# Sums of squares queued one by one between projection products, and a norm's factors spread over the partitions through DRAM

## The chip, the core and the metric

The kernel runs on one core of a Trainium2 chip. The core has five engines with instruction streams of their own: TensorE (PE in the profile, with its weight loads listed as PEld), VectorE (DVE), ScalarE (ACT), GpSimd (POOL) and SyncE (SP), which issues the DMAs of this kernel. They meet through semaphores. The metric is the time of one execution on the device in microseconds (us), as the median of several runs.

## The reference

One inference step of a trunk of two layers over 1152 tokens: 128 context tokens and 1024 latent ones, 9 tiles of 128. A layer normalises its input, projects it, runs three branches (A: windowed attention, B: a linear recurrence, C: differential attention) and merges them. The change touches the end of branch C's heads (4 in a layer, `DV_C` = 128):

```python
def block(qblk):
    s = jnp.einsum('bqhmd,bshmd->bhmqs', qblk, k).astype(jnp.float32) * SCALE
    p = jax.nn.softmax(s, axis=-1)
    pd = p[:, :, 0] - lam * p[:, :, 1]
    return jnp.einsum('bhqs,bshe->bqhe', pd.astype(v.dtype), v)

o = jnp.moveaxis(lax.map(block, qb), 0, 1).reshape(B, T, H_C, DV_C)
o = rmsnorm(o, subln) * (1 - lam_init)
...
oc * jax.nn.silu(g_c)     # the branch's gate, ahead of its output projection
```

Each head's output, a row of 128 numbers for each token, is divided by its root mean square, multiplied by the vector `subln` and a constant, and then by the gate.

## The kernel before

**Layout.** A head's output `u.o` (named `O` in the trace) lies with the 128 features on the partitions and the 1152 tokens along them. The sum of squares of a token therefore runs over the partitions, which a matmul with a column of ones does; it gives nine columns of 128 tokens, tokens on the partitions. The factors have to come back the other way: for each token the same number on all 128 partitions.

**Order.** The unit phase of a layer (`unit_phase`) runs heads 0 to 3 of branch C and then branch A. Each head goes through groups of query tiles: the context tile alone, then pairs of latent tiles. For a group, `q_conv` turns the queries over (transposes L415 into PSUM, ACT and DVE split the result in two halves, `qhl`), `c_probs` makes the scores of a tile (two maps, three blocks of 384 keys each; L513 and L514 on TensorE into `ps_s`), DVE empties each block and takes its maximum (L515), ACT takes exponentials (L525), and DVE joins the two maps (L106). `c_pv`, run a group later from `flush`, transposes the probabilities (L542), ACT and DVE split them (`PT`, L94 and L97), and TensorE multiplies them with the values (`ps_o`, L158 to L160). All of this is written with `tc.high_priority` (offset `HPO` = 2000).

Between groups, `step(n)` advances a generator, `background()`, which feeds projection products for the next head: `tok_gemm` and `ws_chunk` run eight k-steps of `mm3` (three products at L158, L159 and L160, `ps_s<-uwh,h` and `ps_s<-uwl,h`) into one `ps_s` buffer. They fill TensorE while the softmax runs. A scheduler orders the instructions of each engine by priority and dependence, and each engine then runs its own list in that order. Each tile takes a buffer from a ring named by a tag: PSUM has four buffers `s`, three `t` and one `o`; in SBUF the ring `T` (which holds `PT`) has two, `S` 26 and `P` 7.

**A head's end.** `c_finish` (L553 to L571) runs from `flush`, two tiles into the next head. ACT squares `u.o` into `sq` (L555, a `T` buffer). Nine matmuls (L558, `ps_t<-one,sq`, 128 partitions by one column, each two instructions in the trace) make the sums. `rsqrt` runs about a dozen small steps on DVE (`rsq`, 128x9). Nine matmuls with the identity (L566, `ps_t<-ident,rsq`, also two instructions each) spread the factors to all partitions, three to a PSUM buffer. DVE multiplies `u.o` with `subln` and those factors, read from PSUM (L106, called from L568, three of 384 columns), POOL multiplies by the gate, and a DMA on SP's queue stores the head to DRAM (`osp`). Other names that come up: `qkraw`, `qktmp` and `qkss` are the norm of the next head's keys (squares at L365 on ACT, a reduction at L366 on DVE); `qdup` is a doubled copy of the queries (one half by DVE at L410, one by ACT).

Of the kernel before, what the change touches and what calls it, by code (L numbers as in the profile page):

```python
# [10 lines left out]
F32 = mybir.dt.float32  # L11
# [3 lines left out]
ALU = mybir.AluOpType  # L15
# [3 lines left out]
DEPTH = 2  # L19
NTOK = 1152  # L20
NT = 9
KT = 8
# [2 lines left out]

HPO = 2000
TPO = 1500

MLAG = 1
LAG2 = (7, 8)  # L30
# [28 lines left out]
def hybrid_dit_kernel(ctx, tc, I, O):  # L59
# [4 lines left out]
    drp = ctx.enter_context(tc.tile_pool(name="dr", bufs=1, space=bass.MemoryType.DRAM))  # L64
# [3 lines left out]
    def ps(tag, *shape):  # L68
        return psp.tile([128] + list(shape), F32, tag=tag, name="ps_" + tag, bufs=PSB[tag])
# [4 lines left out]
    def al(tag, name, *shape):  # L74

        return big.tile([128] + list(shape), F32, tag=tag, name=name, bufs=RINGS[tag])

    def r(ap):
        return ap.bitcast(F32R)
# [10 lines left out]
    def dma(out, in_):  # L90
        nc.sync.dma_start(out=out, in_=in_)

    def acopy(out, in_, scale=1.0):
        A.activation(out=out, in_=in_, func=AF.Copy, scale=scale)  # L94

    def tt(e, out, a, b, op):
        e.tensor_tensor(out=out, in0=a, in1=b, op=op)  # L97
# [7 lines left out]
    def stt(out, a, s, b, op0, op1):  # L105
        V.scalar_tensor_tensor(out=out, in0=a, scalar=s, in1=b, op0=op0, op1=op1)  # L106

    ident = tl("ident", 128)
    one = tl("one", 1)


    xres = drp.tile([NT, 128, DM], F32, name="xres")
    osp = [drp.tile([4, 128, NTOK], F32, name=f"osp{b}") for b in range(3)]
    xsp, gsp = (drp.tile([4, 128, NTOK], F32, name=n) for n in ("xsp", "gsp"))
    ysp = drp.tile([8, 128, NTOK], F32, name="ysp")
# [3 lines left out]
    def rsqrt(x, n, scale, eps=None):  # L119

        o = tl("rsq", 4, 12, bufs=3)
        ms, y, h, t = (o[:, i, 0:n] for i in range(4))
        if eps is None:
            ts(V, ms, x, scale, ALU.mult, EPS, ALU.add)
        else:
            stt(ms, x, scale, eps, ALU.mult, ALU.add)
        ts(V, y.bitcast(I32), ms.bitcast(I32), 1, ALU.logical_shift_right)
        ts(V, y.bitcast(I32), y.bitcast(I32), -1.0, ALU.mult, float(0x5F3759DF), ALU.add)
        ts(V, h, ms, -0.5, ALU.mult)
        for _ in range(3):  # L130
            tt(V, t, y, y, ALU.mult)
            tt(V, t, t, h, ALU.mult)
            stt(y, t, 1.5, y, ALU.add, ALU.mult)
        return y
# [22 lines left out]
    def mm3(out, lh, ll, rh, rl, first, last):  # L157
        T.matmul(out=out, lhsT=r(lh), rhs=r(rh), start=first, stop=False)  # L158
        T.matmul(out=out, lhsT=r(lh), rhs=r(rl), start=False, stop=False)  # L159
        T.matmul(out=out, lhsT=r(ll), rhs=r(rh), start=False, stop=last)  # L160

    class Lay:
        pass
# [1 line left out]
    def hchunk(L, c, k):  # L165
        return L.hh[k][:, 3 * c:3 * c + 3, :], L.hl[k][:, 3 * c:3 * c + 3, :]

    def ws_chunk(L, hi, lo, c):
        p = ps("s", 384)
        for k in range(KT):  # L170
            a, b = hchunk(L, c, k)
            mm3(p, hi[:, k, :], lo[:, k, :], a, b, k == 0, k == KT - 1)
        return p

    def ws_gemm(L, wcols, consume):
# [173 lines left out]
    def tok_gemm(L, i, w):  # L349
        p = ps("s", 384)  # L350
        for k in range(KT):
            mm3(p, L.hh[k][:, i, :], L.hl[k][:, i, :], w[k][0], w[k][1], k == 0, k == KT - 1)
        return p

    def qk_rows(L, i0, pss, gains, dsts, eng=None):
# [195 lines left out]
        acopy(u.o[:, tiles[0] * 128:tiles[0] * 128 + w], po)  # L551

    def c_finish(L, u, h):  # L553
        sq = al("T", "sq", 1152)
        A.activation(out=sq, in_=u.o, func=AF.Square)  # L555
        p = ps("t", 9)
        for i in range(9):
            T.matmul(out=p[:, i:i + 1], lhsT=sq[:, i * 128:(i + 1) * 128], rhs=one, start=True, stop=True)  # L558
        e2 = tl("e2", 9)
        stt(e2, u.l0, EPS, u.l0, ALU.mult, ALU.mult)  # L560
        y = rsqrt(p, 9, 1.0 / 128, e2)
        for c in range(3):
            pb = ps("t", 3, 128)
            for t in range(3):
                i = 3 * c + t
                T.matmul(out=pb[:, t, :], lhsT=y[:, i:i + 1].to_broadcast([128, 128]), rhs=ident, start=True, stop=True)  # L566
            oc = u.o[:, c * 384:(c + 1) * 384].rearrange("p (t n) -> p t n", t=3)
            stt(oc, oc, L.D.sub1, pb, ALU.mult, ALU.mult)  # L568
            tt(Pq, u.o[:, c * 384:(c + 1) * 384], u.o[:, c * 384:(c + 1) * 384],
               u.gate[:, c * 384:(c + 1) * 384], ALU.mult)  # L570
        dma(osp[2][h], u.o)  # L571

# [126 lines left out]
    def unit_phase(L):  # L701
# [1 line left out]
        l = L.l  # L703
        a_groups = [CQA, CKA, CVA]
        pend = None

        done = None

        def flush():
            nonlocal pend, done  # L710
            d, done = done, None
            if pend:
                pend()
                pend = None
            if d:
                d()

        def start(h):
            u = Unit()
# [21 lines left out]
        def step(n):  # L741
            for _ in range(n):
                next(bg, None)

        def fg(f, *args):
            with tc.high_priority(offset=HPO):
# [431 lines left out]
    for l in range(DEPTH):  # L1178
        L = Lay()
        L.l = l  # L1180
        L.yr, L.ssq, L.units, L.y, L.gates, L.late = [None] * 8, [], [], [], [], []
        L.o = {br: [] for br in range(3)}
        Ls.append(L)

    def drive(*gens):
# [129 lines left out]
```

## Time and profile before

| | |
|---|---|
| median of three runs | 2838.39 us (2835.95 to 2838.65) |
| the profiled execution's own time | 2841.75 us |
| its span in the profile | 2840.0 us |
| mean granted TensorE clock | 0.984 of full speed |
| TensorE busy | 2731.5 us, 96% |
| VectorE busy | 1792.6 us, 63% |
| ScalarE busy | 1285.3 us, 45% |
| GpSimd busy | 923.9 us, 33% |

The rows further down come from one profiled execution. A busy time is the union of an engine's instructions. Matmuls are pipelined: an instruction's listed duration overlaps with the next one's, so the step from one start to the next tells what it costs in a stream. A clock of 1.00 is 2.4 GHz for TensorE; the other level is 1.2 GHz, so a stretch with a mean of 0.90 ran a fifth of its time at that.

### The profile page before, as it was taken

What the parts mean: (1) busy time and instruction counts of PE and PEld (TensorE: products, weight loads), DVE (VectorE), ACT (ScalarE), POOL (GpSimd) and SP (SyncE); (2) the same over time, 40 slices, a digit from 0 to 9 for tenths busy, and PEclk for the clock granted to TensorE, in tenths of its full rate; (3) what the DMA queues carried; (4) which work ended last, traced back from release to release, by engine and by line L of the source; (5) the groups of instructions that cost most, each with busy time, mean ns of one, the idle gap of its engine ahead of it and who ended that gap; (6) DMA issues with size and microseconds to landing.
All of it is one profiled execution on the core that took longest, in us unless ns stands there. A gap on an engine that the chain in (4) does not pass through costs nothing.

```text
span 2840.0 us, 44370 instructions
## 1 busy us (share of the span) xinstructions
PE 2731.5 (96%) x16745; PEld 2640.8 (93%) x16745; DVE 1792.6 (63%) x4412; ACT 1285.3 (45%) x2577; POOL 923.9 (33%) x756
## 2 busy tenths in 40 slices
PE   8999999999999999999999999999999998999999
PEld 4889999999999999999989899999999998999999
DVE  5897878775634675824858887887766257612262
ACT  4464554566635651122244555555666266512200
POOL 1333344541223552122204343445312245512230
PEclk9999999999999999999999999999999999999999
DMA  6010011111222344623531010111122223423232
GB/s 231 26 33 29 24 33 34 35 55 51 89 92 75 112 158 152 199 70 114 173 104 34 24 34 20 33 49 32 49 71 71 90 92 101 163 87 106 76 110 83
DMA packets 240852, 228.52 MB, mean 80 GB/s; under 512 B 22706, under 2 KB 218620, under 8 KB 240636
## 3 DMA queue, kind: packets, MB, share of 16 engines
q1 hardware_dynamic: 240636, 225.67, 24.7%
q8 instruction: 132, 2.16, 0.3%
q14 instruction: 84, 0.69, 0.1%
HBM read 172.40 MB, written 53.22 MB: 79 GB/s over the span
## 4 chain that ended last, share of the span: by engine, by line
PE 73%; DVE 13%; ACT 4%; issue 4%; POOL 2%; DMA 2%; SPq 1%; DVEq 0%; ACTq 0%; POOLq 0%
PE ps_s L158 17%; PE ps_s L159 17%; PE ps_s L160 17%; PE ps_o L159 2%; PE ps_o L158 2%; PE ps_o L160 2%; PE ps_o L684 2%; PE ps_t L675 2%; DVE P L515 2%; PE ps_s L513 2%; PE ps_t L542 2%; PE ps_s L514 1%; DVE lr L907 1%; PE ps_s L635 1%; DVE P L106 1%
## 5 line engine op out<-in xcount | busy, mean ns | idle before, releaser
L158 PE MATMUL ps_s<-h,wsh 128*128 128x384 f32 x1440 | 489.5, 343 | 10.3 <-ACT mg L1005 5.6
L160 PE MATMUL ps_s<-h,wsl 128*128 128x384 f32 x1440 | 485.8, 341 | 1.0 <-POOL wsl L97 1.0
L159 PE MATMUL ps_s<-h,wsh 128*128 128x384 f32 x1440 | 485.8, 340 | 0.0
L97 POOL TENSOR_TENSOR wsl<-wsraw,wsh 128x1024 fp32r<-128x1024 f32 x80 | 199.8, 2497 | 357.5 <-ACT wsh L94 167.1
L158 PEld LDWEIGHTS ps_s<-h,wsh 128*128 128x128 f32 x1440 | 272.0, 189 | 13.6 <-ACT mg L1005 6.6
L160 PEld LDWEIGHTS ps_s<-h,wsl 128*128 128x128 f32 x1440 | 271.3, 189 | 1.9 <-POOL wsl L97 1.6
L159 PEld LDWEIGHTS ps_s<-h,wsh 128*128 128x128 f32 x1440 | 272.1, 189 | 0.3
L97 POOL TENSOR_TENSOR qkraw<-qkraw,tab 128x384 f32<-128x384 f32 (+2 forms) x92 | 132.0, 1446 | 338.7 <-DVE qkraw L97 216.6
L515 DVE TENSOR_SCALAR_CACHE_REDUCE P<-ps_s 128x384 f32<-128x384 f32 (+1 forms) x400 | 205.8, 540 | 38.7 <-PE ps_s L514 37.7
L97 DVE TENSOR_TENSOR PT<-ps_t,PT 128x512 fp32r<-128x512 f32 (+2 forms) x304 | 187.8, 626 | 61.6 <-ACT PT L94 60.0
L158 PE MATMUL ps_s<-uwh,h 128*128 128x384 f32 x648 | 222.7, 345 | 2.9 <-ACT h L94 1.9
L159 PE MATMUL ps_s<-uwl,h 128*128 128x384 f32 x648 | 220.6, 342 | 0.0
L160 PE MATMUL ps_s<-uwh,h 128*128 128x384 f32 x648 | 218.5, 345 | 0.0
L94 ACT ACTIVATE PT<-ps_t 128x512 fp32r<-128x512 f32 (+2 forms) x304 | 159.7, 546 | 127.3 <-PE ps_o L160 69.4
L525 ACT ACTIVATE P<-P,csm 128x1152 f32<-128x1152 f32 (+1 forms) x144 | 165.9, 1155 | 96.0 <-DVE csm L101 96.0
L158 PE MATMUL ps_s<-yh,wsh 128*128 128x384 f32 x480 | 164.0, 347 | 14.9 <-ACT mg L1005 10.2
L1005 ACT ACTIVATE mg<-ps_s 128x384 f32<-128x384 f32 x144 | 69.2, 486 | 239.4 <-DVE ps_s L106 122.6
L158 PE MATMUL ps_s<-woh,yh 128*128 128x256 f32 x576 | 164.0, 286 | 0.0
L160 PE MATMUL ps_s<-yh,wsl 128*128 128x384 f32 x480 | 163.0, 342 | 1.0 <-POOL wsl L97 1.0
L160 PE MATMUL ps_s<-woh,yl 128*128 128x256 f32 x576 | 163.8, 285 | 0.0
L159 PE MATMUL ps_s<-wol,yh 128*128 128x256 f32 x576 | 163.6, 284 | 0.0
L159 PE MATMUL ps_s<-yl,wsh 128*128 128x384 f32 x480 | 162.1, 341 | 0.0
(276 smaller groups left out, 7374.5 us busy)
## 6 DMA issues: line engine op xcount, KB each, us to landing
wsraw<-in_w_in_dram SPq DMA_DIRECT2D x80, 512.0 KB, 4.3
ysp<-yr SPq DMA_DIRECT2D x32, 576.0 KB, 5.6
yr<-ysp SPq DMA_DIRECT2D x32, 576.0 KB, 5.4
wuraw<-in_w_in_dram SPq DMA_DIRECT2D x72, 192.0 KB, 3.9
ol<-osp SPq DMA_DIRECT2D x24, 576.0 KB, 4.9
modw<-in_mod_w_dram SPq DMA_DIRECT2D x20, 576.0 KB, 6.1
modw<-in_mod_w_dram SPq DMA_DIRECT2D x16, 512.0 KB, 5.5
woraw<-in_w_out_dram SPq DMA_DIRECT2D x16, 512.0 KB, 3.4
```

The costliest lines, as they stand in the source:

```text
L94: A.activation(out=out, in_=in_, func=AF.Copy, scale=scale)
L97: e.tensor_tensor(out=out, in0=a, in1=b, op=op)
L158: T.matmul(out=out, lhsT=r(lh), rhs=r(rh), start=first, stop=False)
L159: T.matmul(out=out, lhsT=r(lh), rhs=r(rl), start=False, stop=False)
L160: T.matmul(out=out, lhsT=r(ll), rhs=r(rh), start=False, stop=last)
L513: T.matmul(out=p, lhsT=qh, rhs=kk, start=True, stop=False)
L515: V.tensor_scalar(out=S[:, n * c:n * c + n], in0=p, scalar1=1.0, scalar2=NEG, op0=ALU.mult, op1=ALU.max, accum_out=mx[:, mp, c:c + 1])
L525: A.activation(out=Ss[mp][:, 0:n], in_=Ss[mp][:, 0:n], func=AF.Exp, scale=0.125, bias=nm[:, mp:mp + 1], accum_out=acc)
L542: T.transpose(p[:, b, j * 128:(j + 1) * 128], Pm[:, (b0 + b) * 128:(b0 + b + 1) * 128], ident)
L675: T.transpose(p[:, b, 128 * j:128 * j + 128], Ps[2 * t + j][:, (b0 + b) * 128:(b0 + b + 1) * 128], ident)
L684: T.matmul(out=po[:, t, :, :], lhsT=r(vs[kb]), rhs=r(x[:, b, :]), start=kb + k == 0, stop=k == 1 and kb == len(vs) - 1)
L1005: A.activation(out=m, in_=p, func=AF.Tanh, scale=0.5)
```

## The change

The squares `sq` take a buffer of ring `S` (heads 0 to 2) or `P` (head 3) in place of `T`. The nine sums are no longer written at once: each goes into a list, `L.small`, and a new function `between` takes one out after each k-step of `tok_gemm` and `ws_chunk`; `tc.issue_after` holds it behind the product that was just written. `c_finish` becomes a generator in three parts, advanced one part for each `step` at a priority offset `NPO` = 300, or run to its end by the next `flush`. After the root, the factors are turned by one transpose (9 rows of 128 tokens), copied by ACT into the first nine partitions of `sq`, stored to DRAM (`ybd`, 4.6 KB) and loaded back from there into all of `sq`, the same 1152 numbers to each of 128 partitions (576 KB in SBUF). Both DMAs are on SP's queue. The DVE multiplies then read their factors from `sq` in SBUF. The arithmetic is the same.

```diff
-            mm3(p, hi[:, k, :], lo[:, k, :], a, b, k == 0, k == KT - 1)
+            mm = mm3(p, hi[:, k, :], lo[:, k, :], a, b, k == 0, k == KT - 1)
+            between(L, mm)
...
-            mm3(p, L.hh[k][:, i, :], L.hl[k][:, i, :], w[k][0], w[k][1], k == 0, k == KT - 1)
+            mm = mm3(p, L.hh[k][:, i, :], L.hl[k][:, i, :], w[k][0], w[k][1], k == 0, k == KT - 1)
+            between(L, mm)
...
+    def between(L, mm=None):
+
+        if L.small and mm is not None:
+            with tc.issue_after(mm.ins):
+                L.small.pop(0)()
+        elif L.small:
+            L.small.pop(0)()
...
     def c_finish(L, u, h):
-        sq = al("T", "sq", 1152)
+
+        sq = al("S" if h < 3 else "P", "sq", NTOK)
         A.activation(out=sq, in_=u.o, func=AF.Square)
         p = ps("t", 9)
+
+        def total(i):
+            T.matmul(out=p[:, i:i + 1], lhsT=sq[:, i * 128:(i + 1) * 128], rhs=one, start=True, stop=True)
         for i in range(9):
-            T.matmul(out=p[:, i:i + 1], lhsT=sq[:, i * 128:(i + 1) * 128], rhs=one, start=True, stop=True)
+            L.small.append(lambda i=i: total(i))
+        yield
+        while L.small:
+            between(L)
         e2 = tl("e2", 9)
         stt(e2, u.l0, EPS, u.l0, ALU.mult, ALU.mult)
         y = rsqrt(p, 9, 1.0 / 128, e2)
+        yd = ybd[4 * L.l + h]
+
+        def turn():
+            p = ps("t", 128)
+            T.transpose(p[0:9, :], y, ident)
+            acopy(sq[0:9, 0:128], p[0:9, :])
+            dma(yd, sq[0:9, 0:128])
+            dma(sq.rearrange("p (t n) -> p t n", n=128), yd[None].to_broadcast([128, 9, 128]))
+        L.small += [lambda: None, lambda: None, lambda: None, turn]
+        yield
+        while L.small:
+            between(L)
         for c in range(3):
-            pb = ps("t", 3, 128)
-            for t in range(3):
-                i = 3 * c + t
-                T.matmul(out=pb[:, t, :], lhsT=y[:, i:i + 1].to_broadcast([128, 128]), rhs=ident, start=True, stop=True)
-            oc = u.o[:, c * 384:(c + 1) * 384].rearrange("p (t n) -> p t n", t=3)
-            stt(oc, oc, L.D.sub1, pb, ALU.mult, ALU.mult)
-            tt(Pq, u.o[:, c * 384:(c + 1) * 384], u.o[:, c * 384:(c + 1) * 384],
-               u.gate[:, c * 384:(c + 1) * 384], ALU.mult)
+            cs = slice(384 * c, 384 * c + 384)
+            stt(u.o[:, cs], u.o[:, cs], L.D.sub1, sq[:, cs], ALU.mult, ALU.mult)
+            tt(Pq, u.o[:, cs], u.o[:, cs], u.gate[:, cs], ALU.mult)
         dma(osp[2][h], u.o)
+        yield
...
             if d:
-                d()
+                for _ in fin:
+                    pass
+                fin = d() or iter(())
+                next(fin, None)
...
             for _ in range(n):
                 next(bg, None)
+                with tc.high_priority(offset=NPO):
+                    next(fin, None)
```

The scheduler then places the pieces. The listings below are instructions in the order in which an engine runs them, with the line, the operation and `out<-in`; lines after the change are numbered otherwise (L158 to L160 become L161 to L163, L513 and L514 become L526 and L527, L558 becomes L573, L542 becomes L555). Heads 0 to 2 of both layers have one pattern.

TensorE from the last value product of head 0 of the first layer (`ps_o<-PT,xkv`) on, before the change; `one,sq` are the sums, `uwh,h` and `uwl,h` projection products:

```order
L160 MATMUL ps_o<-PT,xkv 128x128
L558 MATMUL ps_t<-one,sq 128x1 x4
L513 MATMUL ps_s<-ck,qhl 128x384
L558 MATMUL ps_t<-one,sq 128x1
L514 MATMUL ps_s<-ck,qhl 128x384
L558 MATMUL ps_t<-one,sq 128x1 x4
L513 MATMUL ps_s<-ck,qhl 128x384
...
L158 MATMUL ps_s<-uwh,h 128x384
L566 MATMUL ps_t<-ident,rsq 128x128 x9
L159 MATMUL ps_s<-uwl,h 128x384
```

TensorE in the same place after the change, from the last score product to the transpose of the factors:

```order
L527 MATMUL ps_s<-ck,qhl 128x384
L161 MATMUL ps_s<-uwh,h 128x384
L162 MATMUL ps_s<-uwl,h 128x384
L163 MATMUL ps_s<-uwh,h 128x384
L573 MATMUL ps_t<-one,sq 128x1
...
L573 MATMUL ps_t<-one,sq 128x1 x2
...
L163 MATMUL ps_s<-uwh,h 128x384
L586 MATMUL ps_t<-ident,rsq 9x128
L428 MATMUL ps_t<-ident,qdup 128x128
L555 MATMUL ps_t<-ident,P 128x128 x3
```

The sums have moved from the scores to places behind three projection products each, and the nine broadcasts, which stood eleven projection products before the next tiles, have become one transpose that stands behind the last projection product.

ACT at the start of the next group, before the change; the two first rows are the ends of projections, `qktmp` are the squares of the next head's keys:

```order
L94 ACTIVATE uvr<-ps_s 128x128
L94 ACTIVATE qkraw<-ps_s 128x256
L94 ACTIVATE qhl<-ps_t 128x512
L94 ACTIVATE qdup<-uq 128x4x64
L365 ACTIVATE qktmp<-qkraw 128x768
L94 ACTIVATE PT<-ps_t 128x512 x4
```

ACT in the same place after the change:

```order
L96 ACTIVATE uvr<-ps_s 128x128
L96 ACTIVATE qkraw<-ps_s 128x256
L96 ACTIVATE sq<-ps_t 9x128
L378 ACTIVATE qktmp<-qkraw 128x768
L96 ACTIVATE PT<-ps_t 128x512
L96 ACTIVATE qhl<-ps_t 128x512
L96 ACTIVATE qdup<-uq 128x4x64
```

The copy of the turned factors stands first, and the queries' half `qhl` stands behind the squares and a half of the probabilities, where it stood ahead of both.

DVE in the same stretch, before the change; the multiplies by the factors are `O<-O,sub_530,ps_t`:

```order
L106 SCALAR_TENSOR_TENSOR P<-P,csm 128x1152
L106 SCALAR_TENSOR_TENSOR O<-O,sub_530,ps_t 128x384 x3
L410 COPY qdup<-uq 128x4x64
L97 TENSOR_TENSOR qhl<-ps_t,qhl 128x512
L366 TENSOR_REDUCE qkss<-qktmp 128x12
L515 TENSOR_SCALAR P,csm<-ps_s 128x384 x3
```

DVE in the same stretch after the change, where they are `O<-O,sub_531,sq`:

```order
L423 COPY qdup<-uq 128x4x64
L379 TENSOR_REDUCE qkss<-qktmp 128x12
L99 TENSOR_TENSOR PT<-ps_t,PT 128x512
L99 TENSOR_TENSOR qhl<-ps_t,qhl 128x512
...
L99 TENSOR_TENSOR PT<-ps_t,PT 128x512
...
L528 TENSOR_SCALAR P,csm<-ps_s 128x384
L108 SCALAR_TENSOR_TENSOR O<-O,sub_531,sq 128x384 x2
L528 TENSOR_SCALAR P,csm<-ps_s 128x384
L108 SCALAR_TENSOR_TENSOR O<-O,sub_531,sq 128x384
```

The three multiplies have moved from ahead of the copy of the queries to places behind the first and the second emptied block of the next scores.

TensorE at the end of head 3, where branch A follows, before the change:

```order
L558 MATMUL ps_t<-one,sq 128x1 x9
L158 MATMUL ps_s<-uwh,h 128x384
L159 MATMUL ps_s<-uwl,h 128x384
L160 MATMUL ps_s<-uwh,h 128x384
...
L566 MATMUL ps_t<-ident,rsq 128x128 x9
L415 MATMUL ps_t<-ident,qdup 128x128 x4
```

TensorE at the end of head 3 after the change:

```order
L573 MATMUL ps_t<-one,sq 128x1 x9
L162 MATMUL ps_s<-uwl,h 128x384
L163 MATMUL ps_s<-uwh,h 128x384
L586 MATMUL ps_t<-ident,rsq 9x128
L428 MATMUL ps_t<-ident,qdup 128x128
```

Here the nine sums stay in one run; two projection products are left between them and the transpose, where six stood ahead of the broadcasts.

## Rows read from the trace of the kernel before

**Rows 1.** The page: each engine's busy us, share, instructions

```profile
PE 2731.5 (96%) x16745; PEld 2640.8 (93%) x16745; DVE 1792.6 (63%) x4412; ACT 1285.3 (45%) x2577; POOL 923.9 (33%) x756
```

**Rows 2.** Windows, stretches A: span, busy us (instructions) by engine, clock, DMA share

```profile
225.20:243.10 17.90, 17.61 (x102) 16.34 (x101) 13.81 (x50) 6.05 (x12) 8.90 (x15) 0.90 0.01 4
...
1834.40:1850.80 16.40, 16.07 (x102) 15.06 (x101) 13.44 (x50) 5.93 (x12) 8.78 (x15) 1.00 0.02 5
sum 101.90, PE 100.23 PEld 95.40 DVE 81.95 ACT 35.78 POOL 52.91; mean PE 16.71 PEld 15.90 DVE 13.66 ACT 5.96 POOL 8.82
```

**Rows 3.** Windows, the same columns, stretches B

```profile
243.10:253.50 10.40, 10.15 (x71) 9.09 (x69) 9.14 (x31) 4.73 (x11) 0.90 (x1) 1.00 0.15 59
...
1651.20:1662.40 11.20, 11.20 (x85) 11.07 (x83) 10.37 (x35) 5.53 (x12) 1.04 (x2) 1.00 0.16 60
...
sum 63.30, PE 62.05 PEld 56.68 DVE 56.55 ACT 29.35 POOL 5.65; mean PE 10.34 PEld 9.45 DVE 9.42 ACT 4.89 POOL 0.94
```

**Rows 4.** Timeline of TensorE, head 0: start, us, line, op, out<-in, count

```profile
223.13 0.28 PE L158 MATMUL ps_o<-PT,uv 128*128 128x256 f32 x1
223.25 0.28 PE L159 MATMUL ps_o<-PT,uv 128*128 128x256 f32 x1
...
226.33 0.42 PE L513 MATMUL ps_s<-ck,qhl 128*128 128x384 f32 x1
...
226.73 0.42 PE L514 MATMUL ps_s<-ck,qhl 128*128 128x384 f32 x1
...
232.68 0.44 PE L158 MATMUL ps_s<-uwh,h 128*128 128x384 f32 x1
...
239.21 2.17 PE L566 MATMUL ps_t<-ident,rsq 128*128 128x128 f32 x18
241.13 0.42 PE L159 MATMUL ps_s<-uwl,h 128*128 128x384 f32 x1
...
243.13 0.60 PE L415 MATMUL ps_t<-ident,qdup 128*128 128x128 f32 x4
```

**Rows 5.** Timeline of VectorE, head 0

```profile
224.65 0.55 DVE L515 TENSOR_SCALAR_CACHE_REDUCE P<-ps_s 128x384 f32<-128x384 f32 x1
...
225.12 0.55 DVE L515 TENSOR_SCALAR_CACHE_REDUCE P<-ps_s 128x384 f32<-128x384 f32 x1
...
240.29 1.74 DVE L106 SCALAR_TENSOR_TENSOR O<-O,sub,ps_t 128x384 f32<-128x384 f32 x3
```

**Rows 6.** Timeline of all engines, start of stretch B of head 0

```profile
243.76 0.60 ACT L94 ACTIVATE qhl<-ps_t 128x512 fp32r<-128x512 f32 x1
...
244.42 0.97 PE L513 MATMUL ps_s<-ck,qhl 128*128 128x384 f32 x4
244.56 0.84 ACT L365 ACTIVATE qktmp<-qkraw 128x768 f32<-128x768 f32 x1
...
245.30 1.08 ACT L94 ACTIVATE PT<-ps_t 128x512 fp32r<-128x512 f32 x2
245.43 0.95 DVE L366 TENSOR_REDUCE qkss<-qktmp 128x12 f32<-128x768 f32 x1 [0.34 <-ACT qktmp L365]
```

**Rows 7.** DMA issues: out<-in, queue, count, KB each, median us to landing

```profile
ol<-osp SPq DMA_DIRECT2D x24, 576.0 KB, 4.9
...
osp<-O SPq DMA_DIRECT2D x8, 576.0 KB, 2.9
...
out_dram<-uvr SPq DMA_DIRECT2D x10, 64.0 KB, 1.5
```

**Rows 8.** Timeline, end of head 3, both layers; in brackets the wait before

```profile
534.95 0.17 DVE L106 SCALAR_TENSOR_TENSOR rsq<-ps_t,e 128x9 f32<-128x9 f32 x1 [1.95 <-PE ps_t L558]
...
537.51 2.27 PE L566 MATMUL ps_t<-ident,rsq 128*128 128x128 f32 x18 [1.45 <-DVE rsq L106]
537.58 0.96 DVE L97 TENSOR_TENSOR qkraw<-qkraw,rsq 128x768 f32<-128x768 f32 x1
...
1941.25 3.90 PE L566 MATMUL ps_t<-ident,rsq 128*128 128x128 f32 x18 [1.45 <-DVE rsq L106]
```

More of the change, by code (lines that the diff above doesn't have):

```diff
@@ L27 @@
 TPO = 1500
+NPO = 300
 MLAG = 1
@@ L112, in hybrid_dit_kernel @@
     xres = drp.tile([NT, 128, DM], F32, name="xres")
+    ybd = drp.tile([4 * DEPTH, NT, 128], F32, name="ybd")
     osp = [drp.tile([4, 128, NTOK], F32, name=f"osp{b}") for b in range(3)]
@@ L159, in mm3 @@
         T.matmul(out=out, lhsT=r(lh), rhs=r(rl), start=False, stop=False)
-        T.matmul(out=out, lhsT=r(ll), rhs=r(rh), start=False, stop=last)
+        return T.matmul(out=out, lhsT=r(ll), rhs=r(rh), start=False, stop=last)
     class Lay:
@@ L707, in unit_phase @@
         done = None
+        fin = iter(())
         def flush():
-            nonlocal pend, done
+            nonlocal pend, done, fin
             d, done = done, None
@@ L1182, in hybrid_dit_kernel @@
         L.o = {br: [] for br in range(3)}
+        L.small = []
         Ls.append(L)
```

## The prediction

> **What bounds the kernel now.** I read the page's busy times first: TensorE is busy 2731.5 of 2840.0 us [rows 1], so time is saved where TensorE does less, runs at the lower clock less or waits less, and lost where it gets a new wait. Then I cut each of heads 0 to 2 in both layers into two stretches. **Stretch A** runs from the finished head's last value product to the last projection product before the next tiles; it holds the 24 score products of two tiles (12 blocks), the sums, 48 projection products and the broadcasts. **Stretch B** follows, up to the next projection product: scores and value products of the next two tiles. Six stretches A take 101.9 us, and four of the six have a granted clock of 0.90, the other two 1.00 [rows 2]: 0.90 over 17.9 us is some 3.6 us at 1.2 GHz instead of 2.4. Six stretches B take 63.3 us with TensorE busy for 62.05 of them, all at 1.00 [rows 3]. So A has something to give; B has no slack that a new wait could use.
>
> Within A the timeline of TensorE shows the sums in a burst, then the scores, then projection products from 232.68 on, after a wait for VectorE (DVE), which empties the score blocks [rows 4, 5]. DVE needs 0.47 us for a block (225.12 - 224.65) against two products of about 0.17 each: A's first half is bound by DVE, and the burst lies partly under that. This limits what moving the sums can give.
>
> **Stretch A, part by part.** Broadcasts: 18 instructions hold TensorE from 239.21 to 241.13 [rows 4], 1.92 us a head, among projection products at full rate, so all of it counts. One transpose takes their place, 0.12 (as one of those 18, 2.17 us in all with the last's tail). Sums: a sum is two instructions in the trace. Between the scores that begin at 226.33 and 226.73 stands one sum; 0.40 less a score's own 0.17 is 0.23. Nine cost 2.0 between projection products, about what the burst costs now: moving saves nothing of their own time, only what comes after the burst. In the change the scores follow the value products at once. DVE starts at 224.65; a projection product needs one of the four score buffers, so nine blocks must be emptied: 9 x 0.47, and a cast and a small step, 0.4 (an estimate from the 128 columns of the one beside a block's 384). That ends at 229.3; with 0.1 to start it is 4.2 us after 225.20. Then 48 products at 0.176 (37 stand between 232.68 and 239.21), 8.4; sums 2.0; transpose 0.1. Sum 14.7. Six are 88.2. Before they are 101.9, and 0.9 more for five products that in one head already belong to B's window (1651.20): 102.8. **A gives 14.6 us.** The square root's dozen small steps stand behind the softmax on DVE and should end just before the transpose; I cost that at nothing, and 1 us late would cost 1 us a head.
>
> **Stretch B.** Count from the last projection product (243.13 in head 0). Now ScalarE (ACT) makes q's high half at 0.63 and scores start at 1.29 [rows 6]. In the change ACT first copies the turned factors, then squares the keys (0.74 to the next start), copies one transposed tile (0.54) and only then makes q's half. The 9x128 copy is not in the trace: under the 0.54 of a 512-column one, above nothing; I take 0.2, the columns being fewer. q's half ends at 0.63 + 0.2 + 0.74 + 0.54 + 0.6 = 2.7, and scores start at 2.8. TensorE has 12 transposes for that (1.4) and one value product: a new wait of 1.2 us. DVE's part of q follows a 0.95 reduction [rows 6] and two subtractions; the first whole block is there at 5.4, emptied at 5.9. Next on DVE stand two of the three multiplies by the factors (0.6 each [rows 5]; in the change they read SBUF), ahead of the other eleven blocks. Today they lie beside projection products and cost nothing.
>
> They also wait for DRAM. The copy is done at 0.9, SP issues the 4.6 KB store at 1.0, waits for its landing, then issues the load. The store's price is bounded by 1.5 us (64 KB) and 2.9 (576 KB) [rows 7]; I take 1.5, the smaller being nearer. The load, 576 KB with one DRAM row read 128 times, isn't in the trace: 2.9, a store of that size by itself, to 4.9, loads of that size that run several together [rows 7]; I take 3.6, since here it runs alone. It lands at T = 1.0 + 1.5 + 0.1 + 3.6 = 6.2, bounds 5.5 and 8.9. The multiplies start at the later of 5.9 and T. From there until the ninth block is emptied DVE has three multiplies (1.8), eight blocks (3.8), two and a half subtractions of 0.6 (a block's 0.47 for 384 columns, scaled to 512) and small steps (0.3): 7.4. Projection products restart at 13.6. Now it is 10.4, with 8 of 27 value products left for later, 0.12 each [rows 4], which the change does inside: 11.4 in like terms, and 10.3 in the head whose B already holds them (11.2 - 0.9). **B costs** 5 x 2.2 + 3.3 = **14.3 us**. SP waits about 1.5 us for the store; behind it are the head's output store and weight loads whose buffers come free later: nothing, as long as they do.
>
> A rule on this price: the Trainium skill (DMA: Bandwidth & Descriptors, Latency and other measured facts) puts a fixed cost of about 2 us on a DMA to HBM, above the 1.5 of the row. By it T would be 6.7, and the sum would be 3.5 us more, 2846: slower. The row is of this kernel, so it decides.
>
> **Head 3 (twice).** The order shows its nine sums still in one run, two products before the transpose. Now TensorE waits 1.45 us there for DVE [rows 8], and the second time the broadcasts take 3.90 instead of 2.27, 1.6 lost to the lower clock. In the change the chain of small steps, 2.5 us from 534.95 on, gets a 0.96 multiply in between [rows 8]: the factors come 3.4 after the sums, so the wait is 3.0 (more by 1.5); the broadcasts' 2.0 go: 0.5 gained each. A wait of 3 should bring the lower clock if 1.45 did: 1.7 lost in layer 0, nothing new in layer 1. In layer 1 two multiplies stand before the first mask operation, which then comes after T + 1.2 instead of at about 4: some 3 us. Together 4 us lost (0 to 8).
>
> **Sum.** -14.6 + 14.3 + 4 = +3.7 us. The profiled execution took 2841.75 (span 2840.0), 3.4 above the median of the timed runs; the difference goes onto that median, 2838.4: **2842 us**, its own range 2836 to 2848.
>
> **Rivals.** (1) Faster: B's waits don't show, since TensorE finds work or later stretches give the time back; then A alone counts, 2824, or, if all removed TensorE work counts (8 x 1.9 less 8 x 0.12, and 1.8 for each of the four slow stretches), about 2817. For it: TensorE is the busiest engine. Against: B's engines run in order, and B is full now. (2) Slower, late landing: beyond T = 6.2 every us costs 1 us in each of six heads and one or two more, since all blocks of the next scores queue behind the waiting multiply on DVE. At the bound 8.9 that is 2.7 x 7 = 19 more, 2861. For it: the load is issued only after the store has landed; against: few other transfers run there (DMA share 0.15 [rows 3]). It decides from T = 6.4. (3) Slower, clock: B's new waits of 2.5 us bring the 1.2 GHz level there as the burst did in A: 1.8 x 6 = 11 more, 2853. Against: B is at 1.00 in all six now, though almost without waits. The Trainium skill (TensorE: Matmul & The Clock Gate, A second HAM failure mode: psum-queue depth-cycling) tells of short waits for PSUM between groups of matmuls that bring the clock down again and again; rows of A, where a burst and waits stand together, agree. (4) The change doesn't do what it says: true of head 3 alone, by the order, and in the sum.
>
> **How the numbers follow.** Forecast 0.38, faster 0.28, late landing 0.22, clock 0.12. A measurement of this kernel can tell about 0.2% (5.7 us) from no change: faster 0.28, same 0.38, slower 0.34. The range must reach into both sides: 2822 leaves out the faster case's end, 2862 holds the late landing's bound; under 2 in 10 lie outside.
>
> **What would show it.** Right: granted clock 1.00 in every A, some 14.5 us long; scores in B 2.8 us after the last product; B about 13.6 with a wait of TensorE for DVE behind the multiplies; the load landing 6 us after the transpose. Wrong: a B near 11 (rival 1); multiplies waiting for a DMA until 7 or later (rival 2); B with a clock under 0.95 (rival 3); a wait at the transpose in heads 0 to 2, which I cost at nothing.

## The result: 1.0% slower

The changed kernel took 2869.21 us (median of 4 runs, 2868.12 to 2871.74) against 2838.52 of the kernel before beside it: 30.7 us more, ratio 1.0101, 95% interval 1.0079 to 1.0122. The forecast was 2842, the range 2822 to 2862. On another chip, in the experiments below, the same kernel took 2867.80 against 2845.55: 22.3 us more, 1.0071 (1.0054 to 1.0088).

The page of the profile after, beside [rows 1]: TensorE is as busy as before (2731.0 us), in a span of 2870.0 instead of 2840.0. So its idle time has grown by 30.5 us, about as much as the span. Inside the equal busy time two things about cancel (an estimate): the broadcasts that are gone, eight times 1.92 us less a transpose's 0.12, and 24.7 us more at the lower clock, half of which is lost (the traces have 116.3 us at 1.2 GHz for 91.6). DVE is busy for 18.5 us more, ACT for 4.7.

```profile
PE 2731.0 (95%) x16609; PEld 2631.5 (92%) x16609; DVE 1811.1 (63%) x4412; ACT 1290.0 (45%) x2585; POOL 927.2 (32%) x756
```

The windows of the stretches A, from the last value product of a head to the transpose of the factors, with the columns of [rows 2]:

```profile
225.95:240.70 14.75, 14.59 (x85) 12.75 (x84) 12.36 (x48) 6.83 (x12) 6.89 (x12) 1.00 0.02 5
...
1858.30:1872.90 14.60, 14.24 (x83) 12.52 (x83) 12.16 (x47) 6.83 (x12) 6.70 (x13) 1.00 0.02 6
sum 88.75, PE 87.39 PEld 76.74 DVE 74.35 ACT 40.97 POOL 41.63; mean PE 14.57 PEld 12.79 DVE 12.39 ACT 6.83 POOL 6.94
```

And of the stretches B that follow, beside [rows 3]:

```profile
240.70:256.15 15.45, 12.96 (x79) 11.73 (x79) 12.77 (x39) 5.58 (x13) 3.48 (x3) 0.89 0.22 83
343.40:357.05 13.65, 11.92 (x79) 10.11 (x78) 11.69 (x36) 5.79 (x13) 3.48 (x3) 1.00 0.27 93
...
sum 83.50, PE 72.56 PEld 62.29 DVE 71.28 ACT 34.59 POOL 20.90; mean PE 12.09 PEld 10.38 DVE 11.88 ACT 5.77 POOL 3.48
```

All six A are at 1.00 and add up to 88.75 us (88.2 was worked out); five of the B are 13.45 to 13.70 long (13.6), the first, with a drop of the clock in it, is 15.45. So the two stretches did nearly what the prediction said, and most of what it missed must lie elsewhere. To find it, the starts of the same work were laid side by side: TensorE runs 8352 projection products in both kernels, and the start of the n-th after the change, less the start of the n-th before, tells how late the kernel is at that point. The table gives what each part of the program added, in us, for one profiled execution of each kernel (those of the experiments too). The parts end at 218.4, 532.5, 772.0, 1628.7, 1935.2, 2125.4 and 2710.2 us of the kernel before. "Start" and "between" are code that no kernel here changes, but for one or two products. All rows are measured against one execution of the kernel before.

| kernel | start | heads 0-2, layer 0 | head 3, branch A | between | heads 0-2, layer 1 | head 3, branch A | end | sum |
|---|---|---|---|---|---|---|---|---|
| changed | 0.8 | 1.8 | 9.7 | 5.8 | 7.1 | 5.7 | -0.2 | 30.6 |
| again | -2.4 | 1.7 | 9.4 | -0.1 | 7.0 | 5.4 | 0.0 | 21.0 |
| sums_alone | 1.0 | -1.8 | 4.4 | 1.7 | 4.6 | 3.2 | -0.3 | 12.8 |
| spread_alone | 1.5 | 4.4 | 5.5 | 6.0 | 5.8 | 5.4 | -1.3 | 27.2 |
| late_multiply | -1.4 | -6.2 | 5.4 | 4.9 | -0.3 | 7.0 | 0.1 | 9.4 |
| head3_undone | 1.9 | 1.9 | 2.0 | 3.2 | 6.8 | 1.2 | -1.2 | 15.7 |
| root_in_psum | -0.6 | 0.0 | 8.1 | 8.6 | 7.4 | 2.8 | -0.1 | 26.1 |
| late_head3 | 0.9 | -4.4 | 2.4 | 4.3 | 0.6 | -0.3 | -1.4 | 2.1 |
| tied | 1.8 | -10.1 | 2.2 | -1.3 | -5.4 | 1.7 | -0.7 | -11.9 |
| before_tied | -0.6 | -2.8 | -0.2 | -0.6 | 1.3 | -0.2 | -1.2 | -4.2 |
| tied_again | 1.8 | -10.7 | 0.9 | 3.4 | -4.6 | 1.2 | -0.7 | -8.7 |

The changed kernel loses 9 us in heads 0 to 2 and 15 around head 3; in this execution 6 more came in code that the change does not touch.

### The profile page after: what moved, and what is told of

Same layout as the page of the kernel before. It is cut to its first block, busy times and chain, and to the rows that moved or that the text cites. A ratio compares the mean times of both kernels' runs of the same rounds, so it can differ in the third digit from the quotient of the medians.

```text
span 2870.0 us, 44124 instructions
## 1 busy us (share of the span) xinstructions
PE 2731.0 (95%) x16609; PEld 2631.5 (92%) x16609; DVE 1811.1 (63%) x4412; ACT 1290.0 (45%) x2585; POOL 927.2 (32%) x756
## 4 chain that ended last, share of the span: by engine, by line
PE 72%; DVE 12%; DMA 5%; POOL 4%; ACT 3%; issue 3%; SPq 1%; POOLq 0%; ACTq 0%; DVEq 0%
PE ps_s L161 18%; PE ps_s L162 17%; PE ps_s L163 17%; PE ps_o L161 2%; PE ps_o L162 2%; PE ps_o L163 2%; DVE P L528 2%; PE ps_o L712 2%; PE ps_t L703 2%; PE ps_t L555 1%; PE ps_s L526 1%; DVE lr L940 1%; POOL wsl L99 1%; PE ps_s L527 1%; DMA wuraw<-in_w_in_dram 1%
## 5 line engine op out<-in xcount | busy, mean ns | idle before, releaser
L161 PE MATMUL ps_s<-h,wsh 128*128 128x384 f32 x1440 | 490.6, 344 | 13.7 <-ACT mg L1038 6.2
L163 PE MATMUL ps_s<-h,wsl 128*128 128x384 f32 x1440 | 486.7, 341 | 1.0 <-POOL wsl L99 1.0
L161 PEld LDWEIGHTS ps_s<-h,wsh 128*128 128x128 f32 x1440 | 272.7, 190 | 18.0 <-ACT mg L1038 7.2
L163 PEld LDWEIGHTS ps_s<-h,wsl 128*128 128x128 f32 x1440 | 272.0, 189 | 2.0 <-POOL wsl L99 1.6
L161 PE MATMUL ps_s<-uwh,h 128*128 128x384 f32 x648 | 224.8, 349 | 1.9 <-ACT h L96 1.9
L163 PE MATMUL ps_s<-uwh,h 128*128 128x384 f32 x648 | 218.7, 344 | 0.0
L161 PE MATMUL ps_s<-yh,wsh 128*128 128x384 f32 x480 | 164.8, 349 | 16.1 <-ACT mg L1038 11.6
L163 PE MATMUL ps_s<-yh,wsl 128*128 128x384 f32 x480 | 163.6, 343 | 1.0 <-POOL wsl L99 1.0
L161 PE MATMUL ps_s<-woh,yh 128*128 128x256 f32 x576 | 164.3, 286 | 0.0
L163 PE MATMUL ps_s<-woh,yl 128*128 128x256 f32 x576 | 163.7, 285 | 0.0
```

What stands on the lines that cost most here:

```text
L163: return T.matmul(out=out, lhsT=r(ll), rhs=r(rh), start=False, stop=last)
```

## The experiments

Theory "place": the loss comes from work that the change pushed into stretch B and into head 3's end, where TensorE waits for it. Rival "sums": queueing the sums makes the square root end with A, so that whatever follows is late; the way through DRAM adds little. Ratios are to the kernel before on the same chip.

| kernel | us | before | ratio | 95% interval |
|---|---|---|---|---|
| again | 2867.80 | 2845.55 | 1.0071 | 1.0054 to 1.0088 |
| sums_alone | 2853.86 | 2845.55 | 1.0026 | 1.0015 to 1.0038 |
| spread_alone | 2867.98 | 2845.55 | 1.0075 | 1.0055 to 1.0094 |
| late_multiply | 2850.55 | 2845.55 | 1.0016 | 1.0006 to 1.0027 |
| head3_undone | 2858.54 | 2842.67 | 1.0060 | 1.0038 to 1.0081 |
| root_in_psum | 2867.35 | 2842.67 | 1.0088 | 1.0065 to 1.0110 |
| late_head3 | 2843.49 | 2842.67 | 0.9997 | 0.9984 to 1.0010 |
| tied | 2830.11 | 2842.67 | 0.9956 | 0.9941 to 0.9972 |
| before_tied | 2839.12 | 2842.59 | 0.9988 | 0.9975 to 1.0002 |
| tied_again | 2828.69 | 2842.59 | 0.9948 | 0.9929 to 0.9967 |

**again.** No edit.

> The changed kernel once more, nothing edited. Both theories: 2866 to 2872. What it is for: in the first trace of it some 7 us of the loss of 30 lie outside the heads (between 770 and 1500 us after the start, where TensorE's list is the same as before but for one product), and its stretches at the 1.2 GHz level add to 116 us against 92 before. If these belong to the program they are there again, within 2 us; if they are the luck of one execution, the pieces move and the total holds.

2867.80, as expected; but the span of the profiled execution is 2860.3, not 2870.0. By the table the heads and head 3 lose the same in both (8.9 and 8.7; 15.4 and 14.8), while "start" and "between" give 6.6 in one and -2.5 in the other. Time at the lower clock adds up to 116 us in the first and 93 in the second (92 before). So about 24 us of the loss belong to the changed places in both executions, and the rest is not fixed by the program. Whether "between" also loses something on average is not shown: it is over 1 us in eight of the eleven rows, and all of them are compared with the same execution of the kernel before. Nor do the clock's drops explain it by themselves: against the kernel before, "between" has 3.4 us more at the lower clock in the first execution and 10.2 less in the second.

**sums_alone.** The sums stay queued; the broadcasts by matmul come back.

```diff
-        yd = ybd[4 * L.l + h]
-        def turn():
...
-            stt(u.o[:, cs], u.o[:, cs], L.D.sub1, sq[:, cs], ALU.mult, ALU.mult)
+            pb = ps("t", 3, 128)
...
+            stt(oc, oc, L.D.sub1, pb, ALU.mult, ALU.mult)
```

> The sums stay queued between projection products; the factors are spread by nine matmuls and read from PSUM again, right behind the root, for all heads. Theory 'place' (the loss comes from the multiplies and the query half that the round trip through DRAM pushed into stretch B): A still ends at 14.7, the 1.9 us of broadcasts come back, the multiplies read PSUM without waiting for a DMA and stand ahead of the score blocks, so B loses about 1 us instead of 2 to 3: 2838 to 2850. Rival 'sums' (queueing the sums makes the root end with A, so that whatever follows it falls into B; the way through DRAM adds little): 2860 to 2875, as the changed kernel or slower by the broadcasts.

8.3 us slower than before, 14 less than the changed kernel. The windows of its stretches B:

```profile
240.91:254.31 13.40, 12.82 (x97) 12.32 (x96) 12.29 (x39) 5.68 (x11) 3.11 (x3) 1.00 0.14 51
...
sum 80.41, PE 76.84 PEld 73.83 DVE 73.74 ACT 34.07 POOL 18.65; mean PE 12.81 PEld 12.30 DVE 12.29 ACT 5.68 POOL 3.11
```

B is as long as with the DMAs (13.40), although nothing waits for DRAM: the root ends with A, the broadcasts (1.9 us) and the multiplies stand at B's head. That speaks for the rival as to the place of the loss; but here the clock stays at 1.00 through all six heads, where the changed kernel has five drops. The total lies between the two expectations, 4 us above what "place" gave and 6 below what the rival gave, so this run decides for neither.

**spread_alone.** The sums in one run again, with the root and the DMAs behind them.

```diff
-            L.small.append(lambda i=i: total(i))
-        yield
-        while L.small:
-            between(L)
+            total(i)
...
-        L.small += [lambda: None, lambda: None, lambda: None, turn]
-        yield
-        while L.small:
-            between(L)
+        turn()
+        yield
```

> The nine sums in one run again, written at once with the root, the transpose and the two DMAs; only the spreading goes through DRAM. Theory 'place': the multiplies still stand between the score blocks of B and wait there, so 2855 to 2872, B some 13 us long as in the changed kernel. Rival 'sums': with the root early the factors land before B needs them, 2832 to 2845, without a wait of VectorE for the DMA.

22.4 us slower, the whole loss. The rival "sums" as it was put falls: without queued sums the multiplies still stand in B, and the run of sums keeps the clock drops in A (20.5 of 24 us at the lower clock in heads 0 to 2 lie there). The total is the changed kernel's, but it is not made up in the same way: the heads lose 10.2 us and head 3 with branch A 10.9. What this run and sums_alone share is the work in B that DVE does ahead of the score blocks or among them.

**late_multiply.** The three multiplies of heads 0 to 2 behind the last score block of B on DVE.

```diff
-                V.tensor_scalar(out=S[:, n * c:n * c + n], in0=p, scalar1=1.0, scalar2=NEG,
+                L.ev = V.tensor_scalar(out=S[:, n * c:n * c + n], in0=p, scalar1=1.0, scalar2=NEG,
...
+        yield
         for c in range(3):
             cs = slice(384 * c, 384 * c + 384)
-            stt(u.o[:, cs], u.o[:, cs], L.D.sub1, sq[:, cs], ALU.mult, ALU.mult)
+            with tc.issue_after(L.ev.ins):
+                stt(u.o[:, cs], u.o[:, cs], L.D.sub1, sq[:, cs], ALU.mult, ALU.mult)
```

> The changed kernel with one edit: the three multiplies of heads 0 to 2 stand on VectorE behind the last score block of stretch B instead of behind its first and second; everything else as it is. Theory 'place': B falls from 13.6 by the three multiplies (1.75) and the wait for the DMA (0.3 to 1.0), to 11 to 12; six heads give 11 to 15 us, and the waits of the next stretch and some of the clock go too: 2850 to 2860. Rival 'sums': VectorE has the same work, only later, and the loss stays: 2864 to 2872.

5.0 us slower than before, 17.3 less than the changed kernel: "place". Its stretches B, with the same columns:

```profile
337.38:349.06 11.68, 10.95 (x79) 10.45 (x79) 10.02 (x35) 5.59 (x13) 0.00 (x0) 1.00 0.18 58
...
sum 69.98, PE 65.59 PEld 62.59 DVE 60.06 ACT 33.51 POOL 0.00; mean PE 10.93 PEld 10.43 DVE 10.01 ACT 5.59 POOL 0.00
```

B is 11.7 in all six, DVE has 10.0 us of work in it instead of 11.9, and no drop of the clock is left in heads 0 to 2 (17.1 us in the changed kernel, 13.7 before). Two us of DVE's list, moved by ten places, were worth 15 us in heads 0 to 2 (table: 8.7 to 8.9 against -6.5). The edit took the wait for the DMA and the drops of the clock away together with the multiplies, so the 15 us are the worth of the place, not of one of these alone. Head 3, which it leaves as changed, still costs 12.4 us here.

**head3_undone.** Head 3 as before (squares in ring `T`, sums at once, broadcasts, high priority), heads 0 to 2 as changed.

```diff
                 fin = d() or iter(())
                 next(fin, None)
+                if L.old:
+                    for _ in fin:
+                        pass
...
+        if h == 3:
+            for c in range(3):
+                pb = ps("t", 3, 128)
...
```

> The changed kernel with head 3 alone as it was before: sums at once, broadcasts by matmul, at the high priority. In both traces of the changed kernel head 3 and the start of branch A lose some 15 us (9.5 in layer 0, 5.5 in layer 1), where the prediction said 4. Theory 'head 3' (TensorE's wait at the transpose and what it shifts is the cause): 12 to 15 us come back, 7 to 12 slower than the kernel before. Rival 'phase' (heads 0 to 2 shift branch A against GpSimd's conversions, and the collision stays): only the wait at the transpose goes, 2 x 3 with its clock, so 14 to 18 slower than before.

15.9 us slower than before, which by itself is the rival's number; its interval overlaps with that of again, so the total does not decide. The trace does: around head 3 it loses 2.0 and 1.2 where the changed kernel loses 9.5 and 5.5, and the collision in branch A, which is shown further down, is gone. That is "head 3" by the place of the loss. That the total fell by less than the 12 us which that theory gave goes with "start" and "between", 5.1 here against -2.5 in again; what makes them differ is open.

What head 3 does in the changed kernel. DVE, GpSimd and TensorE from their timelines:

```profile
536.52 0.38 DVE L99 TENSOR_TENSOR rsq<-rsq 128x12 f32<-128x12 f32 x2
...
539.16 0.96 DVE L99 TENSOR_TENSOR qkraw<-qkraw,rsq 128x768 f32<-128x768 f32 x1
540.04 0.16 DVE L108 SCALAR_TENSOR_TENSOR rsq<-rsq 128x9 f32<-128x9 f32 x1
540.23 1.86 DVE L99 TENSOR_TENSOR rsq<-rsq 128x9 f32<-128x9 f32 x2
542.13 0.17 DVE L108 SCALAR_TENSOR_TENSOR rsq<-rsq 128x9 f32<-128x9 f32 x1
542.33 1.00 DVE L99 TENSOR_TENSOR rsq<-rsq 128x9 f32<-128x9 f32 x2
543.37 0.52 DVE L108 SCALAR_TENSOR_TENSOR rsq<-rsq 128x9 f32<-128x9 f32 x1
```

```profile
540.26 1.80 POOL L99 TENSOR_TENSOR qkraw<-qkraw,tab 128x768 f32<-128x768 f32 x1 [7.31 <-DVE rsq L108]
542.15 2.26 POOL L99 TENSOR_TENSOR qktmp<-qkraw,tab 128x192 f32<-128x192 f32 x4
```

```profile
538.28 0.33 PE L163 MATMUL ps_s<-uwh,h 128*128 128x384 f32 x1
543.93 0.38 PE L586 MATMUL ps_t<-ident,rsq 128*9 128x128 f32 x1 [5.32 <-DVE rsq L108]
```

The key norm's multiply at 539.16 hands its result to GpSimd, which starts its rotary step at 540.26; from then on two steps of the root, 0.38 elsewhere, take 1.86, until GpSimd's step ends, and two more take 1.00 beside its next steps. Before, that multiply stood behind the root [rows 8], and GpSimd came too late to disturb it.

**root_in_psum.** To try that alone: in head 3 working values of the root lie in PSUM, so that no step reads two tensors from SBUF; the root has four steps more and starts at the same place of DVE's list.

```diff
+        w = ps("t", 2, 12)
...
+        yp, t = (w[:, i, 0:n] for i in range(2))
...
+            tt(V, t, yp, h, ALU.mult)
+            tt(V, t, t, ys, ALU.mult)
```

> The changed kernel; the square root of head 3 alone is written so that each of its steps on VectorE has at most one tensor in SBUF (the working values lie in PSUM), four steps more, in the same places of VectorE's list. Theory 'port' (the root's steps with two SBUF inputs stand still while GpSimd runs the rotary steps of the next keys, 1.86, 1.00 and 0.52 us for pairs and single steps that take 0.38 and 0.17 elsewhere): TensorE's wait at head 3's transpose falls from 5.3 to 3.0 to 3.7, in both layers. Rival 'length' (the wait is the number of steps): it stays at 5.3 or grows by 0.4. In the total 0 to 6 us less than the changed kernel; the two waits are what decides.

The timelines of DVE, GpSimd and TensorE in this kernel:

```profile
535.99 0.96 DVE L99 TENSOR_TENSOR qkraw<-qkraw,rsq 128x768 f32<-128x768 f32 x1
...
537.48 0.38 DVE L99 TENSOR_TENSOR ps_t<-ps_t,rsq 128x9 f32<-128x9 f32 x2
...
538.31 0.39 DVE L99 TENSOR_TENSOR ps_t<-ps_t,rsq 128x9 f32<-128x9 f32 x2
```

```profile
537.10 1.80 POOL L99 TENSOR_TENSOR qkraw<-qkraw,tab 128x768 f32<-128x768 f32 x1 [7.07 <-DVE ps_t L99]
```

```profile
539.04 0.37 PE L604 MATMUL ps_t<-ident,rsq 128*9 128x128 f32 x1 [3.60 <-DVE rsq L108]
```

GpSimd runs its step from 537.10 on, and the root beside it keeps its pace; the wait falls from 5.32 to 3.60 in both layers although the root has four steps more. "Port" holds, "length" falls. The total (0 to 6 us less had been expected) does not move: 24.7 us above the kernel before on its chip, where again was 22.3 above it. Around head 3 it still loses 8.1 us in layer 0, where TensorE waits 1.62 us for the gates at a later place of branch A, and "between" is 8.6 late. So the stall is the cause of 1.7 of the wait's 5.3 us, but not shown to be worth anything in the total.

**late_head3.** late_multiply and head3_undone together.

> Late multiplies for heads 0 to 2 and head 3 as before, together. If the two causes add: heads -9 (as in late_multiply, of which 6.8 is clock), head 3 and branch A 0: 3 to 10 us faster than the kernel before. If the collision in branch A comes back with any shift: 0 to 6 slower.

0.9997 (0.9984 to 1.0010): the loss is gone, but the 3 to 10 us of gain did not come. The number lies where the second expectation put it, yet the collision did not come back: no small step of the key norm is held up in branch A. The heads give 3.8 instead of 9 (the table has 6.5 for late_multiply, and one drop of the clock, 1.7, is back in them), head 3 and branch A cost 2.1, and "start" and "between" 5.2, which no edit explains.

**tied.** late_head3, and `c_pv` held behind the next queries on TensorE and ACT.

```diff
-                    c_pv(L, u, tiles, Ps)
+                    if qi.t is None or g == 4:
+                        c_pv(L, u, tiles, Ps)
+                    else:
+                        with tc.issue_after(qi.t.ins), tc.issue_after(qi.a.ins):
+                            c_pv(L, u, tiles, Ps)
```

> As late_head3, and the transposes and copies of the probabilities are held behind those of the next queries, so that ScalarE makes the queries' first half ahead of them, as it did before. Theory 'ScalarE order' (1.2 us of what is left in stretch B is the queries' half that comes late): B falls from 11.8 to 10.6 to 11.2, 3 to 7 us less than late_head3 over six heads. Rival (TensorE only trades waits, since the value products then come later): B plus the next stretch stays, within 2 us of late_head3.

0.9956: 12.6 us less than the kernel before. But not by the reason given: its B is 11.5 to 11.6 long, 0.1 less than in late_head3 (10.6 to 11.2 had been expected). The first scores still wait for ACT, which turns to the queries only after the factors' copy and the keys' squares:

```profile
242.13 1.05 PE L558 MATMUL ps_t<-ident,P 128*128 128x128 f32 x8
243.81 0.96 PE L529 MATMUL ps_s<-ck,qhl 128*128 128x384 f32 x4 [0.63 <-ACT qhl L96]
```

By the starts of the projection products, 9.5 of the 11.7 us that the heads gain over late_head3 lie behind B (1.7 of them is late_head3's drop of the clock). Why that stretch is shorter was not tried apart.

**before_tied** is that edit on the kernel before; **tied_again** repeats tied beside it.

> The kernel before with one edit: the transposes and copies of the probabilities held behind those of the next queries. tied was 13 us faster than late_head3, but its stretch B did not get shorter (11.75 against 11.85). If the edit pays by itself, wherever the scheduler had the probabilities ahead of the queries: 4 to 12 us faster than the kernel before. If it only mends the order that the change brought: within 3 us of it, and the change's parts carry the gain of tied.

> The same kernel as tied, beside before_tied on one chip: 8 to 14 us faster than the kernel before if the first measurement holds, and that much less before_tied's own gain is what the queued sums, the way through DRAM and the late multiplies are worth together.

0.9988, an interval that just holds no change and a number between the two expectations, against 0.9948, as expected. By the medians the edit by itself is worth 3.5 of the 13.9 us (at the interval's end 7). The rest needs the edit together with the queued sums, the way through DRAM and the late multiplies, head 3 left as it was; neither has it alone: late_head3, which is those parts without the edit, gains nothing.

## Why the prediction was wrong

**Stretch A** was right: 88.75 us for 88.2, all at 1.00. The sums between the products cost what they cost in the run; the broadcasts' 1.92 us are gone, and the root ended just before the transpose in heads 0 to 2, without a wait.

**Stretch B** was right to the half microsecond in five of the six heads, and so were its terms; the sixth, 1.9 longer, has a drop of the clock in it. DVE and SP in head 1 of layer 0; the transpose starts at 343.40:

```profile
344.31 0.30 SPq L93 DMA_DIRECT2D ybd<-sq  x1
345.59 0.33 SPq L93 DMA_DIRECT2D sq<-ybd  x1
```

```profile
348.46 0.56 DVE L528 TENSOR_SCALAR_CACHE_REDUCE P<-ps_s 128x384 f32<-128x384 f32 x1 [0.23 <-PE ps_s L527]
...
349.33 1.15 DVE L108 SCALAR_TENSOR_TENSOR O<-O,sub,sq 128x384 f32<-128x384 f32 x2 [0.30 <-DMA sq<-ybd]
```

The store takes 1.28 us until the load is issued (1.5 were taken), the load 3.7 (3.6); T is 5.9 (6.2). Only head 0 of layer 0 has a slower store (2.28) and T = 6.7. The Trainium skill (DMA: Bandwidth & Descriptors, Latency and other measured facts) has a fixed cost of about 2 us, by which the prediction had worked out another sum. Five of the six stores, at 1.26 to 1.28, lie below it, the sixth above. Rival 2 is the outcome by its sign, but not by its mechanism: DVE's wait for the load is 0.1 to 0.4 us in five heads and 1.05 in the sixth. And sums_alone, with no DMA at all, has a B of 13.40.

**The first step that failed** is that the sum ends with B: "A gives 14.6" went in whole, with what the low clock had cost in four stretches A [rows 2], and the stretch behind B was put at nothing without a reason. Rival 3 looked for the clock in B alone, with 0.12. In four of five cases it came back behind B. Windows of that stretch in head 1 of layer 0, changed and then before:

```profile
376.00:381.40 5.40, 3.66 (x19) 2.63 (x17) 3.91 (x11) 4.38 (x7) 2.65 (x1) 0.87 0.43 126
381.40:386.00 4.60, 4.54 (x21) 4.54 (x22) 4.60 (x15) 2.04 (x4) 2.67 (x1) 0.78 0.05 16
```

```profile
375.00:378.80 3.80, 3.22 (x24) 2.91 (x23) 2.22 (x9) 2.62 (x4) 1.32 (x1) 1.00 0.51 148
378.80:383.00 4.20, 4.20 (x25) 4.20 (x26) 4.20 (x18) 4.05 (x7) 1.37 (x2) 1.00 0.02 5
```

TensorE stands there 1.62 us for the probabilities, where it stood 0.58 before, and then runs at 0.78 (the first row is from the changed kernel, the second from the kernel before):

```profile
378.72 0.39 PE L161 MATMUL ps_o<-PT,uv 128*128 128x256 f32 x1 [1.62 <-ACT PT L96]
378.62 0.39 PE L158 MATMUL ps_o<-PT,uv 128*128 128x256 f32 x1 [0.58 <-ACT PT L94]
```

Before, heads 0 to 2 have four drops of 3.4 us, all in A. After the change there are five (four in again): one in B of head 0, the others behind B, none in A. Each costs 1.7, half its length. The heads lost 8.9 us where -0.3 was worked out, so the miss is 9.2: the five drops make 8.5 of it. In again the miss is 9.0, and the four drops make 6.8; what is left, 0.7 and 2.2, was not taken apart. late_multiply has no drop in any of the six heads, with A 1.2 us longer in all, and sums_alone has none with a B of 13.40, so neither the short A nor the long B brings them. Where the multiplies stand does: with them among the score blocks the heads have three to five drops (changed, again, head3_undone, root_in_psum), with them behind none or one (late_multiply, late_head3, tied, tied_again). That the longer wait brings each drop is read from the order of the rows, not tried by itself.

**The second** is head 3, put at 4 us for both layers (0 to 8). Of its terms, the wait at the transpose was put at 3.0 and is 5.3. The 2.3 are the root's steps that stood still beside GpSimd; root_in_psum takes 1.7 of them away. The prediction read the order of DVE's list there and missed what the key's multiply starts on GpSimd, since on TensorE and DVE nothing shows it. The rest of the loss around head 3, which is gone too in head3_undone, was not taken apart. In layer 0 a collision in branch A belongs to it. GpSimd, DVE and TensorE there:

```profile
599.50 2.39 POOL L99 TENSOR_TENSOR wsl<-wsraw,wsh 128x1024 fp32r<-128x1024 f32 x1 [4.01 <-ACT wsh L96]
```

```profile
599.72 2.21 DVE L105 TENSOR_SCALAR rsq<-qkss 128x6 f32<-128x6 f32 x1
601.96 0.99 DVE L103 TENSOR_SCALAR rsq<-rsq 128x6 int32<-128x6 int32 x2
```

```profile
604.61 0.33 PE L663 MATMUL ps_s<-xkv,qhl 128*128 128x128 f32 x1 [1.72 <-DVE gate L108]
...
606.82 0.69 PE L161 MATMUL ps_s<-h,wsh 128*128 128x384 f32 x1 [1.77 <-DVE gate L108]
```

A step of six columns waits out a weight conversion, the pair after it a multiply by the gate on GpSimd, the gates on DVE queue behind them, TensorE waits 1.7 and 1.8 and runs at the lower clock after that (0.79 from 608 to 618). The same step takes 2.2 us in again, and in layer 1 of spread_alone and of late_multiply, at the places where the table shows 5 to 9 us. In every kernel here whose head 3 goes through DRAM some small step of this norm stands for 0.8 us or more in both layers; where head 3 spreads its factors by matmuls none does.

The kernel before has a stall at the same conversion too, but of another step, a pair that takes 0.74 in the changed kernel. It costs nothing there: TensorE is busy for all 10.00 us from 590 to 600.

```profile
593.26 2.92 DVE L101 TENSOR_SCALAR PA<-PA,asm 128x384 f32<-128x384 f32 x2
593.23 2.40 POOL L97 TENSOR_TENSOR wsl<-wsraw,wsh 128x1024 fp32r<-128x1024 f32 x1 [3.21 <-ACT wsh L94]
```

So what a stall costs depends on what queues behind it.

Rival 4 was right for head 3: its sums did stay in one run. The sum thus missed 9 us in the heads and 11 at head 3; the other 6 of the first execution, in "start" and "between", were not there in the second. The range was too narrow because each term was given its own bounds, and none for what can happen in code that is not touched: by the table "between" alone is -1.3 to 8.6 us in one execution.

## What to carry to other kernels

A gain from a higher clock in one stretch counts only if no later stretch gets a new wait; count the drops over the whole phase, before and after. When a change lets small steps on one engine slip behind a step that feeds another engine, look at what that other engine then does beside them. And when work is taken off the busiest engine, place what is left of it by hand: the same change lost 0.7 to 1.0%, broke even with the multiplies ten places later and head 3 left alone, and won 0.4 to 0.5% with one more order changed.

## What the runs showed of the hardware

DVE steps that read two tensors from SBUF stand still while GpSimd runs an elementwise step: a pair of 128x9 products took 1.86 us beside GpSimd's 1.80, and 0.38 without it; with one of the inputs in PSUM the pair took 0.38 beside the same 1.80. The Trainium skill (SBUF — State Buffer, SBUF: two separate sides) states this as an exclusive lock on a shared pair of ports, held for the whole instruction; these rows agree. Two inputs are not needed: the 128x6 step that stood for 2.21 us beside the 2.39 of the conversion is a tensor-scalar with one tensor in SBUF. The pair without GpSimd, in head 1 of the changed kernel:

```profile
341.50 0.38 DVE L99 TENSOR_TENSOR rsq<-rsq 128x9 f32<-128x9 f32 x2
```

It also bears on the multiplies, whose factors the change moved from PSUM to SBUF: three took 1.74 before [rows 5] and take 2.43 in late_multiply, where GpSimd multiplies by the gate beside the second and third (DVE, then GpSimd):

```profile
350.77 2.43 DVE L108 SCALAR_TENSOR_TENSOR O<-O,sub,sq 128x384 f32<-128x384 f32 x3
351.53 3.51 POOL L99 TENSOR_TENSOR O<-O,gate 128x384 f32<-128x384 f32 x3 [21.91 <-DVE O L108]
```

Two executions of one kernel differed by 23 us in the time that TensorE spent at 1.2 GHz (116 and 93 us) and by 9.7 us in their spans.
